# A mixer projection with the key block first and the values as 2x2 blocks: three of eight value pairs with seven products

## The chip, the cores and the metric

One Trainium2 chip, one of its cores. The metric is the device time of one call of the layer in microseconds, as the median of the runs. A profile of one more execution stands beside it; times inside the program are counted from the start of that profile's span.

## The reference

One encoder layer on 256 tokens of width 2048, all in float32. The change lies in the first part of the mixer, the projection of the normalised input by `w_mix_in` (2048 x 6656):

```
h = rms_norm(x, pre_norm_mix)
q_h, i_h, f_fwd, f_bwd, g_h, q_a, k_a, v_a = split(h @ w_mix_in)
#   columns: q_h 0, i_h 1024, f_fwd 2048, f_bwd 3072, g_h 4096 (1024 each),
#            q_a 5120 (1024), k_a 6144 (256), v_a 6400 (256)
y_h = hgrn2(q_h, i_h, f_fwd, f_bwd, g_h, ...)   # i_h: the values
y_a = window_attention(q_a, k_a, v_a, ...)      # keys and values of two heads
x = x + rms_norm(concat(y_h, y_a) @ w_mix_out, post_norm_mix)
```

Ahead of it and behind it stand a SwiGLU layer each (2048 to 2 x 5632 and back).

## The kernel before

**Products.** Every float32 matrix product is made of three products of rounded parts: each operand is split into a high part `h` and the remainder `l`, and `h*h`, `h*l` and `l*h` are summed in the same PSUM bank. Weights arrive as tiles `raw` of 128 x 2048 (1 MB, three buffers) on SP's queue. Each half of a tile is split by `split_half` (L171) through `split_act` (L176): ScalarE casts the half to `h` (L177), then VectorE subtracts, `l = raw - h` (L178). There are five buffers each for `h` and `l`, so a cast also waits until TensorE has left the half five before. A weight tile's buffer is loaded again once VectorE has made the last `l` from it.

**The input.** `xt` holds x times the gain, transposed, as 16 blocks of 128 rows of k with a high and a low part, in two tiles of eight blocks. It is not yet divided by the norm: the per-token factor `rs2` (one number per token, two columns for the token halves m = 0 and 1) is applied to results. Where a result has the tokens on partitions it is a scale of the eviction; where tokens lie along the free dimension, `spread` (L284) makes a 128 x 256 tile R with `rs2` along the free dimension by one product with a matrix of ones, and R is multiplied in. The two SwiGLU layers do more: `power_and_rest` splits `rs2` into a power of two and a rest, so that multiplying the second token half of `xt` by the exact ratio of the two powers ("evening", L1106) lets the halves be added to one another.

**The mixer's first stage.** The SwiGLU layer's `finish` already multiplies the first eight k-blocks of the first value group by weights that it loaded (`LeadN`: 512 columns from 1024). The mixer then runs, in this order: statistics of x (`pre_stats`) and the constants `lower_bounds`; the other eight blocks of that value group; the second value group (512 columns from 1536); 512 columns from 6144, which are k_a and v_a. These are plain products (`products_N`, L371): for each k-block and token half three products of 128 x 512, so 48 for half a group and 96 for a group. Then `headpair` (L1625) begins with the gates of head pair 0, with the weights as the stationary operand. The order of instructions is the scheduler's, by source order and readiness; `with tc.manual_schedule()` fixes it to the source's, for the engines named.

**Seven products.** `Blocks` (L418) can compute a pair u of k-blocks in another way: the 256 x 256 part of `xt` times the 256 x 1024 part of the weights is seen as 2 x 2 blocks and done with seven block products in place of eight (`seven`, L479), each of three parts. Its cost is sums: of weight blocks on VectorE (L486, L490, L492) between three splits of halves and one of a single block, and of `xt` blocks (`sums_of`, L406, and one split), kept in `sums`. Four partial products gather in banks of their own and are folded into the results at the end (`fold`, L530). The output projection by `w_mix_out` uses this for two of its eight pairs, the SwiGLU layers for many.

Of the kernel before, what the change touches and what calls it, by code (L numbers as in the profile page):

```python
# [11 lines left out]
F32 = mybir.dt.float32  # L12
F32R = mybir.dt.float32r
# [4 lines left out]
ALU = mybir.AluOpType  # L18
AX = mybir.AxisListType

P = 128
D = 2048
T = 256
# [14 lines left out]
def hymba_layer_kernel(  # L38
# [137 lines left out]
    def split_act(hi, lo, src):  # L176
        nc.scalar.copy(hi, src)  # L177
        nc.vector.tensor_tensor(lo, src, hi.bitcast(F32), ALU.subtract)  # L178
# [62 lines left out]
    def pre_stats():  # L241
        with tc.issue_after(last["act"].ins):
            pre_stats_now()
# [37 lines left out]
        nc.vector.tensor_scalar(rest[:, 1:2], rest[:, 1:2], two[:, 0:1], None, ALU.mult)  # L281
        nc.vector.tensor_copy(rest[:, 0:1], rs2[:, 0:1])

    def spread(factor=rs2, n=2):  # L284

        ps = pb()
        for m in range(n):
            nc.vector.tensor_scalar(
                R[:, m * P : (m + 1) * P], ident, factor[:, m : m + 1], None, ALU.mult
            )  # L290
        nc.tensor.matmul(ps[:, : n * P], ones, R[:, : n * P], start=True, stop=True)
        nc.vector.tensor_copy(R[:, : n * P], ps[:, : n * P])


    def xcol(xt, k, part=None):
# [313 lines left out]
    class Pairs(Blocks):  # L609
# [26 lines left out]
        def source(self, u):  # L636
            return Pairs.part(self.w, u, self.now)
# [12 lines left out]
        def left_sums(self, u):  # L650
            if self.ready and u in self.ready:
                return self.ready.pop(u)
            if u in self.kept:
                return self.kept[u]
            keep = self.now == 0 and u in self.keep
            if keep and u in self.near:
                w = self.room.tile([P, 4, 2, P], F32R, tag="sp", name=nm("sp"), bufs=3)
            else:
                tag = f"sp{u}" if keep else "sp"
                w = far["pool"].tile([P, 4, 2, P], F32R, tag=tag, name=nm("sp"), bufs=1 if keep else 2)  # L660
            split_act(w[:, :, 0, :], w[:, :, 1, :], self.sums[u])
            if keep:
                self.kept[u] = w
            return w
# [13 lines left out]
        def folded(self):  # L678
            if self.now == 0:
                wide = self.room.tile([P, 2, 512], F32, tag="sp", name=nm("y"), bufs=3)  # L680
                y = [
                    [
                        self.room.tile([P, 512], F32, tag="z", name=nm("y")),
                        self.room.tile([P, 512], F32, tag="s", name=nm("y")),
                    ],
                    [wide[:, i, :] for i in range(2)],
                ]
            else:
                t = self.post.tile([P, 2, 2, 512], F32, tag="tmp", name=nm("y"), bufs=1)
# [245 lines left out]
    def pair_of(xt, u):  # L935
        return xt[u // 4][:, u % 4 * 2 : u % 4 * 2 + 2]

    class Gated(Blocks):


# [127 lines left out]
    def ffn(gated, w_dn, post_gain, again, gain=None, lead=None, aside=None):  # L1068

        with ExitStack() as st:  # L1070
# [31 lines left out]

            def even(u):

                x = gated.tiles[u].rearrange("p k i t -> p (k i) t")[:, :, P:T]
                nc.vector.tensor_tensor(  # L1106
                    x, x.bitcast(F32), R[:, None, 0:P].to_broadcast([P, 4, P]), ALU.mult
                )

            def sums_in(u):  # L1110
                x = gated.tiles[u].bitcast(F32)
# [428 lines left out]
    def again_from(src):  # L1540
# [17 lines left out]
    cols = later["cols"]  # L1558
# [3 lines left out]
    with ExitStack() as s2:  # L1562
# [33 lines left out]
        w_in = w_mix_in[0]  # L1596
        vh = mid.tile([P, 2, 1024], F32, tag="vh", name="vh")
        for cg in range(2):
            sl = [pa(), pa()] if cg else vbanks
            if cg == 0:  # L1600
                pre_stats()
                with tc.issue_after(last["rs2"].ins):
                    lower_bounds()
            proj_N(w_in, 1024 + cg * 512, 512, xt, sl, k0=0 if cg else 8)
            for m in range(2):
                nc.scalar.mul(
                    vh[:, m, cg * 512 : (cg + 1) * 512], sl[m], rs2[:, m : m + 1]
                )

# [43 lines left out]
        va = mid.tile([P, 2, 256], F32, tag="va", name="va")  # L1653
        kz = mid.tile([P, 2, 256], F32, tag="q", name="kz")
        for m in range(2):
            nc.scalar.mul(kz[:, m, :], sl[m][:, :256], rs2[:, m : m + 1])
            nc.scalar.mul(va[:, m, :], sl[m][:, 256:], rs2[:, m : m + 1])
        kT = mid.tile([P, 2, T], F32, tag="kT", name="kT")

        def turned_keys():  # L1660
# [386 lines left out]
```

## Time and profile before

| | |
|---|---|
| median of 3 runs | 1821.23 us (1820.46 to 1823.14) |
| the profiled execution, time | 1822.32 us |
| its span | 1820.5 us |
| TensorE matmul / weight load busy | 1807.6 / 1501.9 us of the span |
| VectorE / ScalarE / GpSimd busy | 1604.3 / 1137.0 / 162.9 us |
| mixer's value and key groups in the span | about 703.7 to 772.8 us |
| DMA, mean over the span | 246 GB/s |

Matmul rows overlap in the pipeline: a 128 x 512 row lasts 389 ns but the next starts after about 227 ns, so durations are not added up; the distance of starts is. For VectorE and ScalarE, too, a row's end lies a little behind the next start when the next does not depend on it. "Idle before, releaser" is the time for which an engine stood before a row, and what ended it.

### The profile page before, as it was taken

What the parts mean: (1) busy time and instruction counts of PE and PEld (TensorE: products, weight loads), DVE (VectorE), ACT (ScalarE), POOL (GpSimd) and SP (SyncE); (2) the same over time, 40 slices, a digit from 0 to 9 for tenths busy, and PEclk for the clock granted to TensorE, in tenths of its full rate; (3) what the DMA queues carried; (4) which work ended last, traced back from release to release, by engine and by line L of the source; (5) the groups of instructions that cost most, each with busy time, mean ns of one, the idle gap of its engine ahead of it and who ended that gap; (6) DMA issues with size and microseconds to landing.
All of it is one profiled execution on the core that took longest, in us unless ns stands there. A gap on an engine that the chain in (4) does not pass through costs nothing.

```text
span 1820.5 us, 23469 instructions
## 1 busy us (share of the span) xinstructions
PE 1807.6 (99%) x8420; PEld 1501.9 (82%) x8420; DVE 1604.3 (88%) x2075; ACT 1137.0 (62%) x1508; POOL 162.9 (9%) x155
## 2 busy tenths in 40 slices
PE   9999999999999999999999999999999999999998
PEld 7888888888888888888888888888888888888886
DVE  7999999999989989477687798899999999999987
ACT  7565666666666657476587556656666666566663
POOL 1011111111011100000000000101111111011110
PEclk9999999999999999999999999999999999999999
DMA  8889999998699995655554456889999998699894
GB/s 302 236 238 285 276 283 256 249 265 249 218 342 271 294 307 189 199 180 176 165 174 149 164 208 239 253 246 265 281 276 267 256 249 249 193 345 302 265 317 157
DMA packets 212196, 447.59 MB, mean 246 GB/s; under 512 B 11768, under 2 KB 46928, under 8 KB 211312
## 3 DMA queue, kind: packets, MB, share of 16 engines
q1 hardware_dynamic: 180000, 384.87, 61.0%
q0 software_dynamic: 31904, 60.96, 19.5%
q8 instruction: 66, 1.08, 0.2%
q14 instruction: 50, 0.41, 0.1%
q10 hardware_dynamic: 176, 0.27, 0.0%
HBM read 433.46 MB, written 12.60 MB: 245 GB/s over the span
## 4 chain that ended last, share of the span: by engine, by line
PE 94%; DVE 2%; ACT 2%; DMA 1%; issue 1%; POOL 0%; DVEq 0%; ACTq 0%; POOLq 0%; SPq 0%
PE pa L454 41%; PE pb L454 35%; PE pa L322 5%; PE pa L327 3%; PE pa L377 2%; PE pa L375 2%; PE pa L376 2%; DMA raw<-in_w_ffn_gate_up_dram 1%; DVE l L178 1%; PE pa L1161 1%; PE pb L1161 1%; ACT h L177 0%; PE pb L1768 0%; PE pb L1742 0%; PE pb L1846 0%
## 5 line engine op out<-in xcount | busy, mean ns | idle before, releaser
L177 ACT CAST h<-raw 128x1024 fp32r<-128x1024 f32 (+1 forms) x867 | 855.1, 1013 | 466.8 <-PE pb L454 151.2
L178 DVE TENSOR_TENSOR l<-raw,h 128x1024 fp32r<-128x1024 f32 (+1 forms) x867 | 987.5, 1170 | 133.9 <-ACT h L177 99.7
L454 PE MATMUL pa<-h,xt 128*128 128x512 f32 x1096 | 384.6, 392 | 0.1
L454 PE MATMUL pb<-h,xt 128*128 128x512 f32 x940 | 336.7, 392 | 0.3 <-DVE pb L1218 0.3
L454 PEld LDWEIGHTS pa<-h,xt 128*128 128x128 f32 x1096 | 205.8, 188 | 44.1 <-DVE xt L233 0.6
L454 PE MATMUL pa<-l,xt 128*128 128x512 f32 x548 | 213.9, 390 | 0.0
L454 PEld LDWEIGHTS pb<-h,xt 128*128 128x128 f32 x940 | 176.4, 188 | 42.4 <-DVE pb L1225 3.6
L454 PE MATMUL pb<-l,xt 128*128 128x512 f32 x470 | 183.2, 390 | 0.0
L997 POOL DMA_DIRECT2D raw<-in_w_ffn_gate_up_dram x78 | 94.6, 1212 | 733.1 <-DVE l L178 642.2
L454 PE MATMUL pb<-h,ht 128*128 128x512 f32 x452 | 159.2, 389 | 0.0
L454 PE MATMUL pa<-h,ht 128*128 128x512 f32 x452 | 159.1, 389 | 0.0
L322 PE MATMUL pa<-xt,h 128*128 128x512 f32 x512 | 124.4, 393 | 0.2 <-ACT h L177 0.2
L454 PEld LDWEIGHTS pa<-l,xt 128*128 128x128 f32 x548 | 103.0, 188 | 20.7 <-DVE l L178 0.9
L454 PE MATMUL pa<-h,xs 128*128 128x512 f32 x312 | 111.6, 389 | 0.0
L322 PEld LDWEIGHTS pa<-xt,h 128*128 128x128 f32 x512 | 93.8, 188 | 18.6 <-ACT h L177 0.6
L454 PE MATMUL pb<-h,xs 128*128 128x512 f32 x312 | 108.7, 389 | 0.0
L454 PEld LDWEIGHTS pb<-l,xt 128*128 128x128 f32 x470 | 88.3, 188 | 16.7
L454 PEld LDWEIGHTS pb<-h,ht 128*128 128x128 f32 x452 | 84.9, 188 | 17.5
L454 PEld LDWEIGHTS pa<-h,ht 128*128 128x128 f32 x452 | 84.9, 188 | 17.5
L454 PE MATMUL pa<-l,ht 128*128 128x512 f32 x226 | 87.9, 389 | 0.0
L454 PE MATMUL pb<-l,ht 128*128 128x512 f32 x226 | 87.9, 389 | 0.0
L1303 POOL DMA_DIRECT2D raw<-in_w_ffn_down_dram x38 | 46.0, 1212 | 371.5 <-DVE la L178 311.3
(297 smaller groups left out, 2575.0 us busy)
## 6 DMA issues: line engine op xcount, KB each, us to landing
raw<-in_w_ffn_gate_up_dram SPq DMA_DIRECT2D x350, 512.0 KB, 5.7
raw<-in_w_ffn_down_dram SPq DMA_DIRECT2D x88, 1024.0 KB, 8.0
raw<-in_w_mix_in_dram SPq DMA_DIRECT2D x52, 1024.0 KB, 5.0
raw<-in_w_ffn_gate_up_dram POOLq DMA_DIRECT2D x78, 512.0 KB, 8.2
raw<-in_w_ffn_down_dram POOLq DMA_DIRECT2D x38, 512.0 KB, 10.1
raw<-in_w_mix_out_dram SPq DMA_DIRECT2D x16, 1024.0 KB, 4.9
ht<-away SPq DMA_DIRECT2D x24, 512.0 KB, 10.4
away<-ht SPq DMA_DIRECT2D x16, 512.0 KB, 6.9
```

Of the source, the lines that this page charges most:

```text
L177: nc.scalar.copy(hi, src)
L178: nc.vector.tensor_tensor(lo, src, hi.bitcast(F32), ALU.subtract)
L322: nc.tensor.matmul(slot[f], weights(hs, kk, f), xcol(xt, k), start=(k == 0), stop=(k == KT - 1))
L327: nc.tensor.matmul(slot[f][:, 0:T], weights(ls, kk, f), xcol(xt, kh * 8 + kk, 0), start=False, stop=False,)
L375: nc.tensor.matmul(dst, xh, h[:, o : o + n], start=(k == 0), stop=False)
L376: nc.tensor.matmul(dst, xh, l[:, o : o + n], start=False, stop=False)
L377: nc.tensor.matmul(dst, xl, h[:, o : o + n], start=False, stop=(k == KT - 1))
L454: nc.tensor.matmul(self.bank(at), lhs, rhs, start=(n == 1), stop=n in (ends, self.of[at]), skip_group_check=n > ends,)
L997: nc.gpsimd.dma_start(raw[:, 0:1024].rearrange("p (k c) -> p k c", k=2), self.source(u, g)[:, :, 1], accum_op=ALU.add,)
L1161: nc.tensor.transpose(bank[:, o : o + P], zs[m][:, k * P : (k + 1) * P], ident)
L1303: nc.gpsimd.dma_start(raws[i][:, 0:1024].rearrange("p (k c) -> p k c", k=2), Pairs.part(w_dn, u, r)[:, :, 512:1024], accum_op=ALU.add,)
```

## The change

The key block goes first. `LeadN` now loads and multiplies the 512 columns from 6144 (k_a and v_a), in banks called `kvbanks`; the mixer finishes that block (k-blocks 8 to 15) and evicts it to `kz` and `va`.

The values become one block of 1024 columns, as a class `Values(Blocks)` over eight pairs u = 0 to 7, in that order. Pairs 3, 5 and 6 are done with seven products, pairs 0, 1, 2, 4 and 7 plainly, and the partial products are folded in during pair 7.

For that, `xt` is evened in the mixer: `spread_begin(ratio, 1)` spreads the ratio of the two powers, `even` multiplies the second token half of each pair, and `value_sums` makes and splits the sums for pairs 3, 5 and 6. From then on the scale of results is `rest` in place of `rs2`: for the values, for R (`spread(rest)` after the values) and for `gates`. The statistics, `rsqrt`, `power_and_rest`, spreading, evening and the sums stand at places that the source gives: all of this lies in one `manual_schedule` block for TensorE, VectorE and ScalarE. `lower_bounds` comes after the last evening.

```diff
-    def spread(factor=rs2, n=2):
+    def spread_begin(factor, n=2):
         ps = pb()
...
         nc.tensor.matmul(ps[:, : n * P], ones, R[:, : n * P], start=True, stop=True)
-        nc.vector.tensor_copy(R[:, : n * P], ps[:, : n * P])
+        return ps[:, : n * P]
+
+    def spread(factor=rs2, n=2):
+        nc.vector.tensor_copy(R[:, : n * P], spread_begin(factor, n))
...
+    def even_half(x):
+        x = x.rearrange("p k i t -> p (k i) t")[:, :, P:T]
+        return nc.vector.tensor_tensor(
+            x, x.bitcast(F32), R[:, None, 0:P].to_broadcast([P, 4, P]), ALU.mult
+        )
...
-    vbanks = [pa(), pa()]
+    kvbanks = [pa(), pa()]
...
-        lead=LeadN(w_mix_in[0], 1024, vbanks),
+        lead=LeadN(w_mix_in[0], 6144, kvbanks),
...
-        for cg in range(2):
-            sl = [pa(), pa()] if cg else vbanks
-            if cg == 0:
-                pre_stats()
-                with tc.issue_after(last["rs2"].ins):
-                    lower_bounds()
-            proj_N(w_in, 1024 + cg * 512, 512, xt, sl, k0=0 if cg else 8)
+        class Values(Blocks):
...
+        def value_sums(u):
+            z, s = (keepy.tile([P, 4, P], F32, tag=f"sy{i}", name=nm("vs"), bufs=1) for i in range(2))
+            x = pair_of(xt, u).bitcast(F32)
+            whole = z.rearrange("p j t -> p (j t)").rearrange("p (k t) -> p k t", k=2)
+            nc.vector.tensor_tensor(whole, x[:, :, 0, :], x[:, :, 1, :], ALU.add)
+            w = keepy.tile([P, 4, 2, P], F32R, tag=f"yt{VALUES.index(u)}", name=nm("xs"), bufs=1)
+            split_act(w[:, :, 0, :], w[:, :, 1, :], sums_of(whole, s))
+            values.sums[u] = w
+
+        VALUES = (3, 5, 6)
...
+        with tc.manual_schedule(engines=ordered):
+            late = [load(source_N(w_in, 6144, 512, kc)) for kc in (2, 3)]
+            parts = [split(late[0]), ([], [])]
...
             for m in range(2):
-                nc.scalar.mul(
-                    vh[:, m, cg * 512 : (cg + 1) * 512], sl[m], rs2[:, m : m + 1]
-                )
+                for q in (2, 3):
+                    square_x(m, q)
+            rs = [rsqrt_of(squared.pop(m)[0], 1.0 / D, EPS) for m in range(2)]
+            next_half(0)
+            for m in range(2):
+                nc.vector.tensor_copy(rs2[:, m : m + 1], rs[m])
+            power_and_rest()
+            next_half(1)
+            values.begin(range(KT // 2))
+            raw = load(values.source(0))
+            kv(2, 0)
+            kv(2, 1)
+            kv(3, 0)
+            bank = spread_begin(ratio, 1)
+            first = [split_half(raw, 0)]
+            nc.vector.tensor_copy(R[:, :P], bank)
+            even(0)
+            first.append(split_half(raw, 1))
+            even(1)
+            kv(3, 1)
+            for m in range(2):
+                nc.scalar.mul(kz[:, m, :], kvbanks[m][:, :256], rs2[:, m : m + 1])
+                nc.scalar.mul(va[:, m, :], kvbanks[m][:, 256:], rs2[:, m : m + 1])
+            values.play(0, *zip(*first))
+            values.pos = 1
+            values.work(2)
+            even(2, 3)
+            value_sums(VALUES[0])
+            values.work(4)
+            even(4, 5)
+            values.work(5)
+            value_sums(VALUES[1])
+            values.work(6)
+            evened = even(6, 7)
+            for u in VALUES[2:]:
+                value_sums(u)
+            values.work(KT // 2)
+            for m in range(2):
+                for n in range(2):
+                    nc.scalar.mul(
+                        vh[:, m, n * 512 : (n + 1) * 512], values.c[m][n], rest[:, m : m + 1]
+                    )
+        spread(rest)
+        with tc.issue_after(evened.ins):
+            lower_bounds()
...
-        sl = [pa(), pa()]
-        for i, _ in enumerate(proj_N_pieces(w_in, 6144, 512, xt, sl)):
-            if i == 16:
-                spread()
...
-                by = rs2[:, m : m + 1]
+                by = rest[:, m : m + 1]
```

`Values` gives `Blocks` the columns 1024 to 2047 of `w_mix_in` as its source, the sums as `left_sums`, and four rooms for `fold`.

How the order of instructions moves, at two places. First VectorE, in the middle of the values. Before, between two evictions of the projection, its list there holds nothing but remainders of weight halves (`l`, from `raw` and `h`):

```order
L178 TENSOR_TENSOR l_6531<-raw_6528,h_6530 128x1024
L178 TENSOR_TENSOR l_6535<-raw_6528,h_6534 128x1024
L178 TENSOR_TENSOR l_6570<-raw_6567,h_6569 128x1024
L178 TENSOR_TENSOR l_6574<-raw_6567,h_6573 128x1024
L178 TENSOR_TENSOR l_6617<-raw_6614,h_6616 128x1024
```

Now, from the sums for pair 5 (`vs`, `xs`) through pair 5 (`raw_6535`) to the first block of pair 6 (`raw_6588`); L490, L494 and L496 are the sums of weight blocks, L945 the evening of two pairs, L1630 and L412 to L416 the sums of `xt`:

```order
L178 TENSOR_TENSOR xs_6529<-vs_6527,xs_6529 128x4x128
L178 TENSOR_TENSOR l_6538<-raw_6535,h_6537 128x512
L490 TENSOR_TENSOR raw_6535<-raw_6535 128x1024
L178 TENSOR_TENSOR l_6543<-raw_6535,h_6542 128x1024
L494 TENSOR_TENSOR raw_6535<-raw_6535 128x512
L178 TENSOR_TENSOR l_6548<-raw_6535,h_6547 128x1024
L496 TENSOR_TENSOR raw_6535<-raw_6535 128x512
L178 TENSOR_TENSOR l_6553<-raw_6535,h_6552 128x1024
L945 TENSOR_TENSOR xt_5939<-xt_5939,R 128x4x128 x2
L1630 TENSOR_TENSOR vs_6579<-xt_5939 128x512
```

What took two rows of 1024 per weight tile takes seven for a pair with seven products, with the evening and the sums of `xt` in the same list between pairs 5 and 6.

Second ScalarE, at the end of the key block. Before, the key block stood last, and its evictions (L1656, L1657) lay between casts for tiles far behind it:

```order
L177 CAST h_1203_6664<-raw_1202_6662 128x1024
L1656 ACTIVATE kz_6602<-pa_1171_6458,scales_111 128x256
L1657 ACTIVATE va_6601<-pa_1171_6458,scales_111 128x256
L177 CAST h_1205_6668<-raw_1202_6662 128x1024
L1656 ACTIVATE kz_6602<-pa_1172_6459,scales_111 128x256
L1657 ACTIVATE va_6601<-pa_1172_6459,scales_111 128x256
```

Now they stand after the casts for value pair 0 (`raw_1153`) and ahead of those for pair 1 (`raw_1159`); `xs_1166` is the sums' high part for pair 3, `raw_1167` pair 2:

```order
L177 CAST h_1157_6320<-raw_1153_6273 128x1024
L1682 ACTIVATE kz_6218<-pa_41_356,scales_111 128x256
L1683 ACTIVATE va_6217<-pa_41_356,scales_111 128x256
L1682 ACTIVATE kz_6218<-pa_42_357,scales_111 128x256
L1683 ACTIVATE va_6217<-pa_42_357,scales_111 128x256
L177 CAST h_1160_6367<-raw_1159_6365 128x1024
L177 CAST h_1162_6371<-raw_1159_6365 128x1024
L177 CAST xs_1166_6404<-vs_1165_6402 128x4x128
L177 CAST h_1168_6412<-raw_1167_6410 128x1024
```

All four evictions are together, and the casts of pair 1 are queued behind the last of them; the cast of the sums for pair 3 is queued ahead of the casts of pair 2.

More of the change, by code (lines that the diff above doesn't have):

```diff
@@ L1103, in even @@
             def even(u):
-                x = gated.tiles[u].rearrange("p k i t -> p (k i) t")[:, :, P:T]
-                nc.vector.tensor_tensor(
-                    x, x.bitcast(F32), R[:, None, 0:P].to_broadcast([P, 4, P]), ALU.mult
-                )
+                even_half(gated.tiles[u])
             def sums_in(u):
@@ L1597, in hymba_layer_kernel, with source, left_sums, folded @@
         vh = mid.tile([P, 2, 1024], F32, tag="vh", name="vh")
-        for cg in range(2):
-            sl = [pa(), pa()] if cg else vbanks
-            if cg == 0:
-                pre_stats()
-                with tc.issue_after(last["rs2"].ins):
-                    lower_bounds()
-            proj_N(w_in, 1024 + cg * 512, 512, xt, sl, k0=0 if cg else 8)
-            for m in range(2):
-                nc.scalar.mul(
-                    vh[:, m, cg * 512 : (cg + 1) * 512], sl[m], rs2[:, m : m + 1]
-                )
+        class Values(Blocks):
+            def source(self, u):
+                return Pairs.part(w_in, u, 1)
+            def left_sums(self, u):
+                return self.sums[u]
+            def folded(self):
+                return [
+                    [y[:, n, :] for n in range(2)]
+                    for y in (
+                        keepy.tile([P, 2, 512], F32, tag=f"yt{4 + m}", name=nm("y"), bufs=1)
+                        for m in range(2)
+                    )
+                ]
@@ new lines, in hymba_layer_kernel, with next_half, kv, even @@
+        VALUES = (3, 5, 6)
+        values = Values({u: pair_of(xt, u) for u in range(KT // 2)}, dict.fromkeys(VALUES))
+        va = mid.tile([P, 2, 256], F32, tag="va", name="va")
+        kz = mid.tile([P, 2, 256], F32, tag="q", name="kz")
+        ordered = {mybir.EngineType.PE, mybir.EngineType.DVE, mybir.EngineType.Activation}
+        with tc.manual_schedule(engines=ordered):
+            late = [load(source_N(w_in, 6144, 512, kc)) for kc in (2, 3)]
+            parts = [split(late[0]), ([], [])]
+            def next_half(i):
+                for part, of in zip(parts[1], split_half(late[1], i)):
+                    part.append(of)
+            def kv(kc, m):
+                hs, ls = parts[kc - 2]
+                for kk in range(4):
+                    products_N(
+                        xt, kvbanks, m, kc * 4 + kk, hs[kk // 2], ls[kk // 2], kk % 2 * 512, 512
+                    )
+            def even(*us):
+                for u in us:
+                    done = even_half(pair_of(xt, u))
+                return done
+            for m in range(2):
+                for q in (2, 3):
[39 more added lines that the diff above has]
+                        vh[:, m, n * 512 : (n + 1) * 512], values.c[m][n], rest[:, m : m + 1]
+                    )
@@ L1646, in headpair @@
             return z
-        sl = [pa(), pa()]
-        for i, _ in enumerate(proj_N_pieces(w_in, 6144, 512, xt, sl)):
-            if i == 16:
-                spread()
[L1653 to L1657, printed above, removed]
         kT = mid.tile([P, 2, T], F32, tag="kT", name="kT")
```

## The prediction

> **What bounds the kernel now.** First the page: the busy shares, the granted clock and the chain of waits.
>
> ```profile
> span 1820.5 us, 23469 instructions
> PE 1807.6 (99%) x8420; PEld 1501.9 (82%) x8420; DVE 1604.3 (88%) x2075; ACT 1137.0 (62%) x1508; POOL 162.9 (9%) x155
> PEclk9999999999999999999999999999999999999999
> PE 94%; DVE 2%; ACT 2%; DMA 1%; issue 1%; POOL 0%; DVEq 0%; ACTq 0%; POOLq 0%; SPq 0%
> ```
>
> TensorE is busy nearly all of the span at full clock, and 94% of the chain that ended last is its own work. So a product taken away is worth its place in the stream, and any wait put into that stream is paid in full. Next the windows of the changed stage: the end of the first value group, then everything up to the first head pair (columns: length, then busy time of TensorE, weight loads, VectorE, ScalarE, GpSimd, the clock, DMA share, GB/s). Then the groups of splits in this stretch.
>
> ```profile
> 717.80:728.90 11.10, 11.10 (x52) 9.20 (x51) 9.37 (x26) 9.97 (x22) 1.10 (x2) 1.00 0.89 285
> 728.90:772.80 43.90, 43.90 (x196) 36.35 (x195) 20.50 (x21) 20.48 (x22) 0.00 (x0) 1.00 0.61 199
> ...
> L178 DVE TENSOR_TENSOR l<-raw,h 128x1024 fp32r<-128x1024 f32 x22 | 26.8, 1223 | 23.7 <-ACT h L177 23.1
> L177 ACT CAST h<-raw 128x1024 fp32r<-128x1024 f32 x21 | 22.2, 1062 | 19.5 <-PE pa L377 19.5
> ```
>
> From 728.9 TensorE is busy without a gap for 43.9 us, while VectorE and ScalarE work under half of it. VectorE waits for casts and the casts wait for TensorE to release buffers: both run ahead as far as five buffers let them. This is the room that the change draws on.
>
> **What the change removes on TensorE.** The two value groups are 192 products of 128 x 512. Now five plain pairs make 5 x 24 = 120 and three pairs 3 x 21 = 63, so 183: nine fewer. The key block's 96 stay. The second window gives the pitch: 43.9 us for 192 products and one spread of about 0.3 is 0.227 each. Nine are **-2.04 us**. One spread of 128 columns is added:
>
> ```profile
> 1152.07 0.38 PE L291 MATMUL pb<-R,ones 128*128 128x128 f32 x2
> 1152.20 0.47 PE L454 MATMUL pb<-h,xt 128*128 128x512 f32 x1
> 1152.52 0.40 PE L454 MATMUL pb<-l,xt 128*128 128x512 f32 x1
> ```
>
> In the SwiGLU layer the same spread and the product behind it take 0.45 us where the product alone takes 0.23: **+0.22**. The product side gives -1.8 us; that is all there can be won.
>
> **What it adds on VectorE.** Rows of the same operations, from the output projection (a pair with seven products) and from the second SwiGLU layer (evening and sums):
>
> ```profile
> 1048.58 1.23 DVE L178 TENSOR_TENSOR l<-raw,h 128x1024 fp32r<-128x1024 f32 x1 [0.21 <-ACT h L177]
> 1049.72 1.22 DVE L486 TENSOR_TENSOR raw<-raw 128x1024 f32<-128x1024 f32 x1
> 1050.85 0.69 DVE L178 TENSOR_TENSOR sp<-sy,sp 128x512 fp32r<-128x512 f32 x1
> 1051.45 0.68 DVE L490 TENSOR_TENSOR raw<-raw 128x512 f32<-128x512 f32 x1
> 1052.11 1.23 DVE L178 TENSOR_TENSOR l<-raw,h 128x1024 fp32r<-128x1024 f32 x1
> 1053.25 0.69 DVE L492 TENSOR_TENSOR raw<-raw 128x512 f32<-128x512 f32 x1
> ...
> 1081.62 0.68 DVE L178 TENSOR_TENSOR la<-raw,ha 128x512 fp32r<-128x512 f32 x1
> 1082.34 1.22 DVE L486 TENSOR_TENSOR raw<-raw 128x1024 f32<-128x1024 f32 x1
> ...
> 1152.48 0.29 DVE L292 COPY R<-pb 128x128 f32<-128x128 f32 x1
> 1152.81 2.50 DVE L1106 TENSOR_TENSOR xt<-xt,R 128x512 fp32r<-128x512 f32 x4
> 1155.23 0.69 DVE L1113 TENSOR_TENSOR z<-xt 128x512 f32<-128x512 f32 x1
> 1156.43 0.42 DVE L408 TENSOR_TENSOR s<-z 128x256 f32<-128x256 f32 x1
> 1158.70 0.28 DVE L412 TENSOR_TENSOR s<-z,s 128x128 f32<-128x128 f32 x1
> 1158.91 1.22 DVE L178 TENSOR_TENSOR l<-raw,h 128x1024 fp32r<-128x1024 f32 x1
> ```
>
> From start to start a row of 1024 takes 1.13 us (1049.72 to 1050.85), one of 512 takes 0.60 (1050.85 to 1051.45), 256 about 0.34, 128 about 0.20 (1158.70 to 1158.91). A row that needs the one before takes 0.12 more (1081.62 to 1082.34).
>
> The list from the first evening to the last remainder of pair 6: eight evenings at 0.60, 4.8; eight halves of plain pairs (pair 0's second, two each of pairs 1, 2, 4, pair 7's first) at 1.13, 9.0; three pairs with seven products, each 0.60 for the first block, 1.13 + 0.60 + 0.60 for sums and 3 x 1.13 for halves, so 6.3, together 19.0; three sums of `xt` at 0.60 + 0.34 + 0.20 + 0.20 + 0.60 = 1.9, 5.8; the small rows of the bounds and one of R, about 0.7, my estimate from the 128 row. Together **39.3 us**.
>
> TensorE's need: the key block's remaining 48 products begin at 717.83,
>
> ```profile
> 717.83 0.48 PE L375 MATMUL pa<-h,xt 128*128 128x512 f32 x1
> ```
>
> so values begin at 717.83 + 10.9 + 0.2 = 728.9. The last remainder of pair 6 is read behind 154 value products, 34.9 us later, at 763.8. VectorE begins evening at about 727.0: the spread product cannot run before 726.0 (36 products in) and the copy of R takes 0.29 behind it, and VectorE's own queue (the split remainders 1.13 x 3 and some ten small statistics rows behind the last gain of `xt`) ends at the same point. It is done at 766.3 if it never waits: **2.5 us late**, from throughput alone.
>
> **The waits in that list.** These rows give the hand-offs:
>
> ```profile
> 773.00 0.47 ACT L1656 ACTIVATE kz<-pa,scales 128x256 f32<-128x256 f32 x1 [0.31 <-PE pa L377]
> 773.37 0.47 ACT L1657 ACTIVATE va<-pa,scales 128x256 f32<-128x256 f32 x1
> ...
> 1047.49 1.05 ACT L177 CAST h<-raw 128x1024 fp32r<-128x1024 f32 x1 [0.98 <-PE pa L454]
> 1054.03 1.05 ACT L177 CAST h<-raw 128x1024 fp32r<-128x1024 f32 x1 [1.00 <-DVE raw L492]
> ```
>
> A remainder starts 1.09 us after its cast of 1024 (1047.49 to 1048.58), a cast 0.1 after the sum that it waits for (1053.25 + 0.69 to 1054.03). So: (a) the casts of pair 1 stand behind the eviction of the key block's second half, which waits for its last product at 728.9; casts begin near 729.9, VectorE, done with pair 0 at 729.3, waits 1.6. (b) Each sum of `xt` sends VectorE to ScalarE and back (0.77), with the next pair's casts queued behind that cast (0.36), and three or four of its steps depend on the one before (0.36 to 0.48): pair 3 pays all of it, 1.6; for pair 5 the next cast stands ready, 1.1; for pair 6 the bounds' rows lie between the steps as well, 0.9. (c) In pairs 3 and 5 the last half is cast only after the last sum of weight blocks and nothing else stands in VectorE's list: 1.2 and two dependent steps, 1.45 each; pair 6 has pair 7's first half there, 0.1. Together 1.6 + 3.6 + 3.0 = **8.2 us**.
>
> TensorE then waits 2.5 + 8.2 = **10.7 us**. Laid out pair by pair, pairs 0 to 3 still arrive in time (pair 3's last remainder with some 0.9 us to spare), pair 4 is just late (0.2), pair 5 costs about 3, pair 6 about 7.5, with the longest single wait near 3 us at pair 6's first block. Pair 7's splits are then ready. None of it is made good later, since TensorE is never idle for want of anything but work.
>
> **Edits costed at nothing.** The statistics and the scale's split go ahead of the key block's last quarter on VectorE: that block's second half needs its remainder at about 725.0 and gets it at 724.8 to 725.2, so 0 to 0.3, and what it costs there is no longer missing later, since VectorE's list is what runs late. Loads: a tile of `w_mix_in` lands 5.0 us after its issue,
>
> ```profile
> raw<-in_w_mix_in_dram SPq DMA_DIRECT2D x52, 1024.0 KB, 5.0
> ```
>
> each is released by a remainder three tiles back, and pair 6's is issued when pair 3 is split, some 18 us before pair 6's casts; on SP's queue nothing but the same loads and the early bias rows stands ahead. Evictions of values, 4 x 0.69 on ScalarE, lie under the first head pair. The fold is eight rows of 0.60 on VectorE under pair 7 and the head pair; its first two results free the bank that the head pair's second product needs, by my layout 0.9 us before TensorE asks. If that cover is gone it costs up to 2.5 us (four rows of 0.60). The moved bounds cost ScalarE a table load in a stretch where it waits for VectorE's sums anyway.
>
> **Sum.** -2.04 + 0.22 + 10.7 = **+8.9 us**. Against the profiled execution's own 1822.32 us (span 1820.5 and 1.8 around it) that is 1831.2; against the median of the runs, 1.1 lower, 1821.2 + 8.9 = **1830.1 us**.
>
> Bounds of the unknown part, the waits in VectorE's list: none at all gives 2.5 us of waiting for TensorE; every hand-off at 0.1 more than taken (a dozen of them) and the fold uncovered give 10.7 + 1.2 + 2.5 = 14.4. I take 10.7, since each wait is read from the order of two in-order queues.
>
> **Rivals.**
>
> *The lead holds (not slower).* Mechanism: ScalarE and VectorE enter pair 4 far enough ahead that pairs 5 and 6 arrive in time. For it speaks the output projection, where VectorE is as full and TensorE never waits while a pair of seven is made:
>
> ```profile
> 1047.00:1056.00 9.00, 9.00 (x41) 7.47 (x40) 8.79 (x11) 5.08 (x6) 0.00 (x0) 1.00 0.63 234
> ```
>
> Against it: there the evening and most sums are absent, a plain pair lies between the two pairs with seven, and casts are not held by an eviction. It decides from the point where the lower remainder of pair 5 is ready by 756.4 (121 value products behind 728.9); my layout has it near 757.5. Then only the products count: 1821.2 - 1.8 = **1819.4**.
>
> *Throughput alone.* The queues interleave better than I lay them out and only the 2.5 us remain: 1821.2 - 1.8 + 2.5 = **1821.9**. Against it stand the fixed order in the manual block and the eviction ahead of pair 1's casts.
>
> *The clock drops in a wait.* The kernel's first five products come at a slow pace, and the only long wait of TensorE in the mixer leaves the clock at 1.00:
>
> ```profile
> 1.38 2.31 PE L129 MATMUL pb<-idle 128*128 128x512 bf16 x5 [1.38 <-DVE idle L123]
> ...
> 932.07 1.99 PE L1911 MATMUL pb<-pt,va 128*128 128x256 f32 x8 [0.84 <-ACT pt L1903]
> ...
> 930.00:934.00 4.00, 3.16 (x15) 2.40 (x14) 2.01 (x5) 3.97 (x6) 0.00 (x0) 1.00 0.00 0
> ```
>
> If the wait of 3 us at pair 6 has the effect of the program's start, about eight products come at (2.31 - 0.63) / 4 = 0.42 in place of 0.23 us: 1.5 us, **1831.6**. The Trainium skill (page "TensorE: Matmul & The Clock Gate", section "HAM oscillation — how this bites in real kernels") asks for no gap over about 3.4 us, since the array then runs at half rate; by that rule the wait lies just under the limit, and a drop would cost about 1.7 us as an estimate from its figures. No wait of that length is in this trace.
>
> *The backlog reaches the head pair.* The fold's rows stay behind TensorE and the second bank comes late: 1830.1 + 2.5 = **1832.6**. Against it: 0.9 us of margin.
>
> **How the numbers follow.** Forecast 0.67, lead holds 0.09, throughput alone 0.10, clock 0.06, backlog 0.08. What can be told from no change is about 0.2%, 3.6 us: 1817.6 to 1824.9. Faster than that needs the lead and luck on top: 0.02. Same: most of the first two rivals and the forecast's low end, 0.16. Slower 0.82. The forecast's own range is 1826 to 1833; with throughput alone and the upper bound (1821.2 - 1.8 + 14.4 = 1833.8) the range is 1821.5 to 1834.
>
> **What will show it.** In the new profile: 183 products between the key block and the first head pair; before them none or almost no wait of TensorE; in pairs 5 and 6 waits released by VectorE's `l` and ScalarE's `h`, 3 and 7 us in sum; VectorE over 80% busy from 727 to 774, with waits for `xs` and for the last `h` of pairs 3 and 5; ScalarE's casts of pair 1 right behind the second eviction. I am wrong if pair 5 arrives without a wait, if TensorE waits for a DMA there, or if the waits pass 14 us.

## The result, and the profile after

| | before | after |
|---|---|---|
| time, median of 6 runs | 1821.22 us (1820.46 to 1823.14) | 1832.19 us (1831.11 to 1834.51) |
| ratio | | 1.0058, 95% interval 1.0046 to 1.0071: slower by 0.6% |
| profiled execution: time, span | 1822.32, 1820.5 us | 1832.07, 1830.2 us |
| granted clock, mean | 0.999 | 0.996 |

The forecast was 1830.1 us, range 1821.5 to 1834.0. The page of the changed kernel, with the same four kinds of line as before (the span, the engines' busy time, the granted clock by slice, the shares of the chain of waits):

```profile
span 1830.2 us, 23528 instructions
PE 1811.9 (99%) x8413; PEld 1501.8 (82%) x8413; DVE 1633.9 (89%) x2129; ACT 1143.2 (62%) x1518; POOL 162.9 (9%) x155
PEclk9999999999999999899999999999999999999999
PE 92%; DVE 4%; ACT 2%; DMA 1%; issue 1%; POOL 0%; DVEq 0%; ACTq 0%; POOLq 0%
```

Two things are new: VectorE's share of the chain rose from 2% to 4%, and one slice of the clock shows an 8. Both lie in the value stage. The next rows are the windows of before, then of after, over the same stretch (length, busy time of TensorE, weight loads, VectorE, ScalarE and GpSimd, clock, DMA share, GB/s).

```profile
727.00:774.00 47.00, 47.00 (x209) 38.92 (x208) 22.50 (x28) 23.10 (x28) 0.45 (x1) 1.00 0.62 202
```

```profile
727.00:774.00 47.00, 40.87 (x159) 30.94 (x158) 39.77 (x58) 22.04 (x28) 0.00 (x0) 0.90 0.44 148
728.57:781.92 53.35, 47.22 (x184) 36.08 (x183) 46.08 (x67) 26.53 (x33) 0.00 (x0) 0.90 0.47 154
```

VectorE went from 22.5 to 39.8 of 47 us, 85%, and TensorE is no longer full. The last row is the whole value stage, from its first product to the second spread, with its 183 products. At the pitch of 0.227 us they need 41.5; the stage took 53.35. So TensorE lost **11.8 us** in it. Less the 1.8 that fewer products save, this is +10.0, against +9.75 between the two profiled executions and +10.97 between the medians.

"Lost" is meant like this for every kernel below: length of the stage less products x 0.227. TensorE's busy time in such a row does not serve, since the end of a matmul is modelled and slow products count as busy.

Who is waited for in this stage, first by TensorE (total, times, longest, in us), then the waits of VectorE in its own list (a timeline of the changed kernel: start, duration, what ran, and in brackets the idle time before it and its releaser):

```profile
PE pa L458 <- ACT h L177: 2.8, 1, 2.8
PE pa L458 <- DVE l L178: 2.3, 4, 0.8
PE pb L458 <- DVE l L178: 0.8, 1, 0.8
PE pb L458 <- ACT h L177: 0.3, 1, 0.3
```

```profile
730.59 2.36 DVE L178 TENSOR_TENSOR l<-raw,h 128x1024 fp32r<-128x1024 f32 x2 [1.83 <-ACT h L177]
...
736.67 0.69 DVE L178 TENSOR_TENSOR xs<-vs,xs 128x512 fp32r<-128x512 f32 x1 [0.69 <-ACT xs L177]
...
746.92 1.23 DVE L178 TENSOR_TENSOR l<-raw,h 128x1024 fp32r<-128x1024 f32 x1 [1.48 <-ACT h L177]
...
754.03 0.69 DVE L178 TENSOR_TENSOR xs<-vs,xs 128x512 fp32r<-128x512 f32 x1 [0.69 <-ACT xs L177]
...
761.37 1.23 DVE L178 TENSOR_TENSOR l<-raw,h 128x1024 fp32r<-128x1024 f32 x1 [1.19 <-ACT h L177]
...
766.31 0.69 DVE L178 TENSOR_TENSOR xs<-vs,xs 128x512 fp32r<-128x512 f32 x1 [0.68 <-ACT xs L177]
```

These are the hand-offs (a), (b) and (c) of the prediction, places where VectorE stands until ScalarE has made the cast that it needs. Each is where it was expected: pair 1's casts behind the eviction (1.83), three sums of `xt` (0.69, 0.69 and 0.68), the last halves of pairs 3 and 5 (1.48 and 1.19). No wait of TensorE or VectorE in this stage names a DMA.

The chain of work that ended last says the same. It leaves TensorE at 745.8 and comes back to it at 770.05, and between the two it runs over ScalarE and VectorE alone:

```profile
745.83 1.06 ACT h L177
...
768.86 1.15 DVE l L178
770.01 0.04 issue
770.05 3.78 PE pa L458 x8
```

TensorE's recorded waits add up to 6.2 us, not to 11.8. Most of the rest lies in its slow products, since a low clock, to which the prediction gave a chance of 0.06, came as well. TensorE's timeline at the start of pair 6, and the windows around it:

```profile
763.67 0.40 PE L458 MATMUL pb<-h,xt 128*128 128x512 f32 x1
766.85 0.79 PE L458 MATMUL pa<-h,xt 128*128 128x512 f32 x1 [2.78 <-ACT h L177]
767.66 0.80 PE L458 MATMUL pa<-l,xt 128*128 128x512 f32 x1
768.25 1.05 PE L458 MATMUL pa<-h,xt 128*128 128x512 f32 x2
770.05 0.80 PE L458 MATMUL pa<-l,xt 128*128 128x512 f32 x1 [0.75 <-DVE l L178]
...
771.07 0.63 PE L458 MATMUL pa<-h,xs 128*128 128x512 f32 x1
771.50 0.63 PE L458 MATMUL pa<-l,xs 128*128 128x512 f32 x1
...
775.31 0.40 PE L458 MATMUL pb<-l,xs 128*128 128x512 f32 x1
```

```profile
758.20:761.61 3.41, 2.88 (x12) 1.70 (x10) 2.22 (x4) 1.30 (x2) 0.00 (x0) 1.00 0.00 0
761.61:765.02 3.41, 1.70 (x6) 0.86 (x5) 3.41 (x8) 1.02 (x1) 0.00 (x0) 1.00 0.37 101
765.02:768.43 3.41, 1.57 (x3) 0.97 (x4) 2.69 (x7) 2.42 (x5) 0.00 (x0) 0.50 0.60 206
768.43:771.84 3.41, 2.66 (x7) 1.65 (x6) 3.41 (x6) 1.99 (x2) 0.00 (x0) 0.50 0.02 5
771.84:775.26 3.42, 3.42 (x9) 2.63 (x8) 3.42 (x6) 2.69 (x4) 0.00 (x0) 0.50 0.00 0
```

From 765.0 to 775.3 the granted clock is 0.50, and products start 0.43 us apart (771.07 to 771.50) where 0.227 was the pitch. The sixteen products from 766.85 to 775.31 took 8.5 us; at that pitch they would take 3.6. So two accounts of the 11.8 us stood open: VectorE's list is late, or the halved clock is the cost. The experiments begin there.

### The profile page after: what moved, and what is told of

It reads as the page before. It is cut to its first block, busy times and chain, and to the rows that moved or that the text cites. A ratio compares the mean times of both kernels' runs of the same rounds, so it can differ in the third digit from the quotient of the medians.

```text
span 1830.2 us, 23528 instructions
## 1 busy us (share of the span) xinstructions
PE 1811.9 (99%) x8413; PEld 1501.8 (82%) x8413; DVE 1633.9 (89%) x2129; ACT 1143.2 (62%) x1518; POOL 162.9 (9%) x155
## 4 chain that ended last, share of the span: by engine, by line
PE 92%; DVE 4%; ACT 2%; DMA 1%; issue 1%; POOL 0%; DVEq 0%; ACTq 0%; POOLq 0%
PE pa L458 41%; PE pb L458 36%; PE pa L326 5%; PE pa L331 3%; DVE l L178 2%; PE pa L381 1%; PE pa L380 1%; PE pa L379 1%; DMA raw<-in_w_ffn_down_dram 1%; PE pa L1169 1%; PE pb L1169 1%; ACT h L177 0%; PE pb L1856 0%; PE pb L1830 0%; PE pb L1934 0%
## 5 line engine op out<-in xcount | busy, mean ns | idle before, releaser
L458 PE MATMUL pa<-h,xt 128*128 128x512 f32 x1148 | 403.8, 393 | 2.9 <-ACT h L177 2.8
L458 PE MATMUL pb<-h,xt 128*128 128x512 f32 x986 | 352.8, 392 | 0.0
L458 PEld LDWEIGHTS pa<-h,xt 128*128 128x128 f32 x1148 | 216.1, 188 | 49.3 <-ACT h L177 3.2
L458 PE MATMUL pa<-l,xt 128*128 128x512 f32 x574 | 225.1, 392 | 2.1 <-DVE l L178 2.1
L458 PEld LDWEIGHTS pb<-h,xt 128*128 128x128 f32 x986 | 185.1, 188 | 44.0 <-DVE pb L1233 3.5
L458 PE MATMUL pb<-l,xt 128*128 128x512 f32 x493 | 192.2, 390 | 0.0
L458 PEld LDWEIGHTS pa<-l,xt 128*128 128x128 f32 x574 | 108.1, 188 | 25.7 <-DVE l L178 5.1
L458 PE MATMUL pa<-h,xs 128*128 128x512 f32 x324 | 116.7, 392 | 0.0
L458 PE MATMUL pb<-h,xs 128*128 128x512 f32 x324 | 113.8, 391 | 0.3 <-ACT h L177 0.3
```

The source lines that it names most:

```text
L458: nc.tensor.matmul(self.bank(at), lhs, rhs, start=(n == 1), stop=n in (ends, self.of[at]), skip_group_check=n > ends,)
```

## The experiments

Eleven kernels, each run beside the kernel before. The "lost" column is stage length less products x 0.227; the last column is the difference of medians.

| kernel | products | stage, us | lost, us | median, us | to its own before, us |
|---|---|---|---|---|---|
| the change | 183 | 53.35 | 11.8 | 1832.19 | +11.0 |
| e1, no pair of seven | 192 | 43.53 | 0 | 1822.46 | +0.5 |
| e2, pairs 3 and 6 | 186 | 44.35 | 2.1 | 1823.42 | +1.5 |
| e3, evictions later | 183 | 51.16 | 9.6 | 1830.35 | +8.4 |
| e4, evenings in the hand-offs | 183 | 50.95 | 9.4 | 1830.79 | +8.8 |
| e5, zero products in the wait | 183 + 12 | 53.09 | 11.5 | 1833.20 | +11.6 |
| e6, sums on GpSimd | 183 | 56.80 | 15.3 | 1835.97 | +14.4 |
| e7, sums and evenings on GpSimd | 183 | 53.03 | 11.5 | 1830.98 | +9.4 |
| e8, e3 and e4 together | 183 | 49.11 | 7.6 | 1827.40 | +5.8 |
| e9, e2 with both edits | 186 | 42.17 | 0 | 1821.45 | -0.6 |
| e10, four evenings less | 183 | 50.58 | 9.0 | 1829.25 | +7.2 |
| e11, e7 without its wait for R | 183 | 53.34 | 11.8 | 1831.63 | +9.6 |

### e5: is it the clock?

```diff
+            for _ in range(12):
+                nc.tensor.matmul(
+                    values.c[0][0],
+                    none,
+                    values.sums[5].rearrange("p j i t -> p (j i t)")[:, 0:512],
+                    start=False, stop=False,
+                )
             values.work(KT // 2)
```

`none` is a block of zeros.

> Twelve products of a zero block are put into TensorE's queue between pair 5 and pair 6 (2.7 us at 0.227), where the change waits 2.78 us; they add zero to a bank. Theory (the data of pair 6 comes late, and the slow products only pass time that TensorE would wait anyway; with the clock at 1.00 its last remainder would be used 0.4 us earlier): 1832.2 - 0.4 = 1831.8, and TensorE still waits inside pair 6. Rival E (the halved clock is the cost): 16 products at 0.43 in place of 0.227 us are 3.2 us, so 1829.0.

Measured: 1833.2 us, ratio 1.0065 (1.0048 to 1.0081). The stage of this kernel, and rows of TensorE's timeline in it:

```profile
727.74:780.83 53.09, 47.44 (x196) 35.97 (x195) 45.85 (x67) 26.53 (x33) 0.00 (x0) 1.00 0.47 154
```

```profile
763.11 2.97 PE L1700 MATMUL pa<-xs,none 128*128 128x512 f32 x12
...
769.24 0.50 PE L458 MATMUL pa<-l,xt 128*128 128x512 f32 x1 [1.43 <-DVE l L178]
...
774.12 0.50 PE L458 MATMUL pb<-l,xs 128*128 128x512 f32 x1 [0.76 <-DVE l L178]
```

The long wait is filled, the clock stays at 1.00 through the whole stage, and the stage is shorter by 0.26 us. The filling itself delayed nothing: pair 6's first product came 38.3 us behind the first of the stage in both kernels. So 0.26 us is what the halved clock cost here, by one profile of each kernel: at full speed TensorE reaches each next remainder sooner and waits for it instead (1.43 and 0.76 in these rows). Rival E, 3.2 us, falls. The median did not get better at all.

### e1, e2: which part of the change costs it?

```diff
-        VALUES = (3, 5, 6)
+        VALUES = ()          # e1
+        VALUES = (3, 6)      # e2
```

The calls of `value_sums` follow the list.

> No pair with seven products; the key block first, the spread and the eight evenings stay. Theory (VectorE's list is too long by the sums and hand-offs of the sevens): the list loses 3 x 6.3 + 5.8 and gains six halves of 1.13, about 21 us in place of 39.3, so TensorE never waits in the value stage: 192 products and the spread, 1821.2 + 0.2 = 1821.4 us. Rival A (the new order or the evening costs by itself): 1824 to 1828, with waits of TensorE released by xt or by the eviction.

> Sevens in pairs 3 and 6 alone, two plain pairs between them. Theory: the list falls by 6.3 + 1.9 - 2.3 = 5.9 us, which is more than the 2.5 us that it was late, and the hand-offs of one pair go too; a wait of about 1 us is left at pair 6: 1821.2 - 1.36 + 0.22 + 1.0 = 1821.1 us. Rival B (every pair with seven products costs the same, a third of what the change costs): 2 x (10.97 - 0.22) / 3 = 7.2 more than 1821.4: 1828.6. Rival C (the low clock in the long wait is the cost): no wait over 1 us, clock 1.00 throughout, and the time falls by the whole of it, to 1820.

Measured: e1 1822.46 us, ratio 1.0003 (0.9994 to 1.0012); e2 1823.42, ratio 1.0009 (0.9999 to 1.0018). The stages of e1 and of e2 by windows:

```profile
727.64:771.17 43.53, 43.53 (x194) 36.04 (x193) 25.45 (x32) 22.47 (x26) 0.00 (x0) 1.00 0.66 219
```

```profile
729.54:773.89 44.35, 43.01 (x187) 34.76 (x186) 39.18 (x57) 24.23 (x30) 0.00 (x0) 1.00 0.56 184
```

With the key block first, the statistics ahead of it, the spread and all eight evenings, but no pair of seven, TensorE loses nothing: rival A falls. Two pairs of seven with two plain ones between lose 2.1 us, where a third of the change's loss for each would be 7.9: rival B falls too. So does rival C: in e2 the clock is 1.00 and no wait is over 0.8 us, yet the time is not 1820. The loss is not so much for each such pair; it follows what VectorE has to do in the stage: 39.18 us busy in e2 and 46.08 in the change (row 728.57:781.92), while the products need 42.2 and 41.5. The theory's wait of 1.0 for e2 was too low by 1.1, and its 1821.1 us by 2.3.

### e3, e4, e8: the hand-offs

```diff
             kv(3, 1)
-            for m in range(2):
-                nc.scalar.mul(kz[:, m, :], ...)
-                nc.scalar.mul(va[:, m, :], ...)
             values.play(0, *zip(*first))
             values.pos = 1
             values.work(2)
+            for m in range(2):                       # e3
+                nc.scalar.mul(kz[:, m, :], ...)
+                nc.scalar.mul(va[:, m, :], ...)
```

```diff
-            values.work(4)
-            even(4, 5)
+            values.work(3)
+            with_hole(3, 4, 5)     # e4: pair 3, with even(4, 5) ahead of its last half
             values.work(5)
             value_sums(VALUES[1])
-            values.work(6)
-            evened = even(6, 7)
+            evened = with_hole(5, 6, 7)
```

> Key and value evictions stand behind the casts of pair 1 on ScalarE; all else as in the change. Theory: VectorE's wait of 1.83 us at 730.6 goes, the rest of its list moves up by as much, and TensorE's waits in pairs 4 to 6 fall from 11.7 to about 10: 1832.2 - 1.8 = 1830.4. Rival D (throughput or the buffers set it, the wait is taken again further on): 1832 with the same 11.7.

> The evenings of tiles 4, 5 and 6, 7 stand ahead of the last remainder of pairs 3 and 5 on VectorE, so the hand-off to ScalarE (waits of 1.48 and 1.19 us) has work in it. Theory: 1.2 us each are saved, TensorE's waits fall from 11.7 to about 9.3: 1832.2 - 2.4 = 1829.8. Rival D: the same time as the change, 1832, since the last remainder of pair 5 now comes later by two rows of 0.60.

> The edits of the evictions and of the evenings in one kernel. Alone they shortened the value stage by 2.2 and 2.4 us. Theory: they act at different places of VectorE's list, but pair 3's hand-off no longer lies on the path once the casts come early, so less than the sum: 3.5 to 4.6 us off, 1828.2, with waits of about 7.5 left. Rival D (the same wait is removed by both): 1830.

Measured: e3 1830.35 us, ratio 1.0044 (1.0029 to 1.0059); e4 1830.79, 1.0048 (1.0031 to 1.0065); e8 1827.40, 1.0033 (1.0021 to 1.0045). In the stage e3 wins 2.2 us, e4 2.4, and e8 4.2 of their sum of 4.6. The theory had 1.8, 2.4 and 3.5 to 4.6; the median of e4 came out 1.0 above its forecast, while its stage is as forecast. Each hand-off that is hidden comes back to TensorE nearly whole, further down its stream: VectorE's list is late from pair 4 on, and whatever shortens it shortens the end. Rival D falls.

### e10: four rows less on VectorE

```diff
-            even(2, 3)
...
-            even(4, 5)
```

This kernel leaves out the evening of four of the eight pairs, so its values are not the layer's.

> The evenings of tiles 2 to 5 are left out (the second half of the rows keeps its own scale there), four rows of 0.60 on VectorE and nothing else; every hand-off between the queues stays. Theory (VectorE's list is late from pair 4 on, so each row in it is paid): TensorE's waits fall by 4 x 0.60 = 2.4 from 11.8 to 9.4, 1829.8. Rival I (only the hand-offs set the waits and VectorE has slack between them): the rows are taken up by longer waits for casts, 1832.2. Rival A' (ScalarE's casts wait for TensorE's buffers, so that VectorE's time is worth half): 1831.0.

Measured: 1829.25 us, ratio 1.0043 (1.0027 to 1.0058); the stage is 2.8 us shorter for four rows of 0.60. No hand-off was touched, so rows count as much as waits do, and rivals I and A' fall. It is 0.4 more than the rows; where that came from was not followed up.

### e6, e7, e11: the rows on GpSimd

```diff
-    def sums_of(u, w):
+    def sums_of(u, w, on=nc.vector):
...
-            nc.vector.tensor_tensor(whole, x[:, :, 0, :], x[:, :, 1, :], ALU.add)
+            nc.gpsimd.tensor_tensor(whole, x[:, :, 0, :], x[:, :, 1, :], ALU.add)
...
-                    done = even_half(pair_of(xt, u))                       # e7, e11
+                    done = even_half(pair_of(xt, u), nc.vector if u < 2 else nc.gpsimd)
...
-        spread(rest)                                                       # e11
-        with tc.issue_after(evened.ins):
+        with tc.issue_after(evened.ins):    # here the last remainder of a sum
+            spread(rest)
             lower_bounds()
```

The three other rows of `sums_of` go to GpSimd in the same way, in all three kernels.

> The four rows of each sum of xt stand on GpSimd in place of VectorE; the casts and remainders stay. GpSimd's one row of 128x512 took 1.27 us, VectorE's 0.60. Theory (the order of two in-order queues sets the waits): a sum takes 3.0 us in place of 1.6, ScalarE's cast of it comes later and the casts of the next weights stand behind it, so VectorE waits longer and TensorE's waits rise from 11.8 to 12 to 13: 1833. Rival F (only the length of VectorE's list counts): 5.1 us fewer rows, waits of 6.7, 1827.

> The evenings of tiles 2 to 7 and all sums of xt stand on GpSimd, which is otherwise idle here. They begin at 726.3 and take about 6 x 1.3 + 3 x 2.6 = 15.6 us, so each is done before ScalarE comes to its cast, except the first, at pair 3. Theory: VectorE's list falls from 39.3 by 5.1 + 3.6 to about 30 us, 35 are there; the hand-offs are hidden but for pair 3's; waits of TensorE of 1 to 3 us at pair 6 and none at pair 5: 1821.2 - 1.8 + 2 = 1821.4. Rival G (GpSimd and VectorE slow each other down, so that the rows on either take half as long again): VectorE's rows of 1.13 become longer and the waits stay over 6 us: over 1826.

> As the kernel with evenings and sums on GpSimd, but the second spread and the bounds are issued behind the last remainder of a sum, so that VectorE's queue no longer holds a row that writes R behind GpSimd's reading of it (6.01 us of VectorE's time there). Theory (the shared rows stay slow: 1.22 became 2.3 on VectorE and 1.28 became 2.2 on GpSimd while both worked): the first sum still ends at about 737, so some 2.5 of the 6 us are won: 1828.4. Rival J (the wait for R alone made that kernel slow): waits of 5 to 6 us go, 1825. Rival K (nothing is won, since ScalarE's cast of the first sum comes as late as before): 1831.

Measured: e6 1835.97 us, ratio 1.0077 (1.0062 to 1.0092); e7 1830.98, 1.0051 (1.0036 to 1.0066); e11 1831.63, 1.0054 (1.0040 to 1.0068). All three missed the theory's numbers. e6 lost 15.3 us, more than the 12 to 13 expected; rival F's 6.7 falls. VectorE's wait at pair 3's sum, 0.69 in the change, is 4.02 there:

```profile
737.26 0.69 DVE L178 TENSOR_TENSOR xs<-vs,xs 128x512 fp32r<-128x512 f32 x1 [4.02 <-ACT xs L177]
```

For e7 the theory had 1821.4, and rival G, over 1826, was right. Rows of VectorE and of GpSimd in e7 while both worked:

```profile
725.43 0.69 DVE L945 TENSOR_TENSOR xt<-xt,R 128x512 fp32r<-128x512 f32 x1
726.04 2.32 DVE L178 TENSOR_TENSOR l<-raw,h 128x1024 fp32r<-128x1024 f32 x1
728.27 1.78 DVE L945 TENSOR_TENSOR xt<-xt,R 128x512 fp32r<-128x512 f32 x1
...
737.25 0.46 DVE L288 TENSOR_SCALAR R<-ident,scales 128x128 f32<-128x128 f32 x1 [6.01 <-POOL xt L945]
```

```profile
725.54 5.67 POOL L945 TENSOR_TENSOR xt<-xt,R 128x512 fp32r<-128x512 f32 x3 [5.27 <-DVE lb L1601]
731.17 1.28 POOL L1630 TENSOR_TENSOR vs<-xt 128x512 f32<-128x512 f32 x1
```

Alone, VectorE's remainder takes 1.22 us and the evening 0.69; here 2.32 and 1.78, longer by 1.10 and 1.09, close to one GpSimd row of 1.28 less what overlaps. GpSimd's three evenings take 5.67 where 3 x 1.28 would be 3.8. The two engines take turns on these rows, so where they meet a row given to GpSimd costs VectorE more than the 0.60 that it saved. The Trainium skill (page "SBUF — State Buffer", section "Who interferes with whom") has a rule for this: a VectorE instruction with two SBUF inputs contends with a GpSimd instruction that reads SBUF, for a shared pair of ports that is an exclusive lock. By that rule these rows come out as sums, and the trace agrees (2.32 for 1.13 and 1.28); the number expected for e7 had not reckoned with it.

On top of that VectorE stood 6.0 us behind a row that rewrites `R`. e11 took that wait away, and its stage is no shorter (53.34). The first sum of `xt` now ended even later on GpSimd, ScalarE's casts were queued behind it, and VectorE stood 5.83 us at the sum's remainder instead:

```profile
740.67 1.21 DVE L178 TENSOR_TENSOR xs<-vs,xs 128x512 fp32r<-128x512 f32 x1 [5.83 <-ACT xs L177]
```

Rival K was right there, and rival J falls.

### e9: what is left if the list fits

e2 with the edit of e3, and the evenings of tiles 4 and 5 in pair 3's hand-off.

> Sevens in pairs 3 and 6 alone, the evictions behind the casts of pair 1, the evenings of tiles 4 and 5 in pair 3's hand-off. With the sevens in 3 and 6 alone TensorE still waited 2.1 us (stage of 44.35 less 186 x 0.227). Theory: the two edits took 2.2 and 2.4 us off a list that was late throughout; here 2.1 are left to take, so no waits: 2.1 us under the 1823.4 of the kernel without them, 1821.3, beside the 1821.2 to 1822.0 of the kernel before: no difference that can be told. Rival H (products taken off are won in full once no wait is left, 6 x 0.227 - 0.22 = 1.1 us): 0.06% faster than before, 1820.6.

Measured: 1821.45 us, ratio 0.9996 (0.9988 to 1.0005). Its stage:

```profile
729.41:771.58 42.17, 42.17 (x188) 34.91 (x187) 39.45 (x57) 23.19 (x30) 0.00 (x0) 1.00 0.59 201
```

VectorE is 94% busy and TensorE loses nothing: 186 x 0.227 is 42.2. This is the version that keeps what is won, but the 1.1 us (0.06%) that the products give is not told from no change, so rival H stays undecided. It beats the change by far; that it beats the kernel before is not shown.

## Why the prediction was right

- **Products.** 183 between the key block and the first head pair, and with no waits (e9, e1) the stage is products x 0.227 to within 0.1 us. -2.04 and +0.22 hold as they stand.
- **Start.** Values were to begin at 728.9 and began at 728.57; in front of them TensorE was busy for 26.85 of 27 us (700 to 727) before and after. Statistics ahead of the last quarter cost nothing, as costed.
- **VectorE's list.** First evening at 726.3 (forecast 727.0), end of pair 6's last remainder at about 774.8 (forecast 727.0 + 39.3 + 8.2 = 774.5). That the end fits so well is in part luck: the list began 0.7 earlier than forecast and took 1.0 longer.
- **(a)** forecast 1.6, measured 1.83, and taken away in e3 it gave 2.2. **(b)** forecast 1.6, 1.1 and 0.9 with the dependent steps: measured 1.6, 1.15 and 0.8, from start to start less the rows' own time; the bare waits are 0.69 at each sum and 0.26 at the cast behind the first. **(c)** forecast 1.45, 1.45 and 0.1 with the dependent steps: the bare waits are 1.48, 1.19 and none. Pair 3's is 0.29 longer for a reason that the forecast had not named: its last cast was released at 745.83 by TensorE, which left a buffer then, and not by the sum of weight blocks, which was done about 0.4 before.
- **TensorE's waits by pair**, each pair counted from the end of the one before, less what its products need: pairs 0 to 3 none, pair 4 0.8 (forecast 0.2), pair 5 3.2 (3), pair 6 7.8 (7.5), pair 7 none. The longest single one is 2.8 (near 3), at pair 6's first block, as said.
- **Costed at nothing.** TensorE and VectorE waited for no load. ScalarE did once, 3.25 us up to 780.2, with casts for the head pair behind the values, and TensorE did not wait after it. The fold stayed covered: from 782 to 830 TensorE has no recorded wait, so the backlog rival (1832.6) was near in time and wrong in mechanism.
- **The rivals.** The lead did not hold. Throughput alone did not describe it: hidden hand-offs gave their time back (e8, 4.2 us). The clock rival was half right: the clock fell, at the place named, to 0.50. But its price was worked out from the slow products (1.5 us) as if TensorE had its data; it did not, and e5 puts the price at 0.26. The step that failed is that one: a slow product inside a wait costs only what goes beyond the wait.

The sum was 10.7 of waits and 11.8 came: 0.6 at pair 4, 0.2 at pair 5, 0.3 at pair 6, the last about what the clock cost. The other part of the distance from 1830.1 to 1832.2 lies in the step from profiled runs to medians: the profiled execution of before was 1.1 above its median, that of after 0.1 below.

## What to carry to other kernels

Half-idle is an average: before a change is put under the cover of a busy engine, write down the in-order list of the covering engine up to the last deadline, with every hand-off to another queue in it, and compare its end with the time at which it is needed. Once such a list is late, rows and hand-offs alike are paid in full further on, and the cure is less work in it (two pairs of seven in place of three) or other rows inside the hand-offs, not a faster product side. A helper engine has to be quick enough for the queue behind it (e6), and its rows must not exclude those of the engine that it relieves (e7).

## What the hardware showed beyond that

**The clock changes by stretches of 3.41 us, not by single gaps.** In the change it fell at 765.0 and came back at 775.3, 10.24 us later. In e4, where the longest wait was 1.57 us, it fell as well, at 766.39, while a product ran, and came back 6.83 later. It fell in this stage in eight of the twelve changed kernels, for 3.41 us (e11), 6.83 (e4, e6, e7, e8, e10) or 10.24 (the change, e3): once, twice or three times 3.41. The two windows of e4 ahead of the fall and the first behind it:

```profile
759.57:762.98 3.41, 2.31 (x9) 1.24 (x7) 3.41 (x8) 2.20 (x2) 0.00 (x0) 1.00 0.02 5
762.98:766.39 3.41, 1.54 (x6) 0.67 (x4) 2.69 (x7) 2.42 (x5) 0.00 (x0) 1.00 0.89 303
766.39:769.80 3.41, 2.01 (x5) 1.49 (x5) 3.41 (x6) 1.99 (x2) 0.00 (x0) 0.50 0.02 5
```

TensorE was busy for 1.54 of 3.41 us in the stretch that ended with the fall (1.70 in the change, 0 to 1.74 in the other six); 2.31 and 2.88 in the stretches ahead let it stand, and so did 1.92 in e6 (762.73 to 766.15). So about half of a stretch fits as the limit, as an estimate from these figures. One stretch of e11, the first of these, does not fit:

```profile
737.47:740.88 3.41, 1.53 (x7) 0.94 (x5) 0.21 (x1) 0.86 (x2) 3.33 (x5) 1.00 0.51 210
740.88:744.30 3.42, 1.74 (x6) 1.23 (x7) 3.42 (x3) 3.12 (x4) 2.65 (x3) 1.00 0.01 2
744.30:747.71 3.41, 3.41 (x9) 2.63 (x8) 3.38 (x4) 0.64 (x1) 3.25 (x3) 0.50 0.55 150
```

There 1.53 let the clock stand, and only the 1.74 behind it brought it down. Why is open: the ends of products are modelled, so these shares are rough, and no run set them on purpose. The way back is plainer: in all eight kernels the clock rose behind a stretch in which TensorE was busy throughout (3.42 in the change, where 2.66 in the stretch ahead was not enough).

The rule of the Trainium skill that the prediction named (page "TensorE: Matmul & The Clock Gate", section "HAM oscillation — how this bites in real kernels"), no gap over about 3.4 us, was too mild for the change and e4: their longest recorded waits were 2.78 and 1.57 us and the clock fell all the same, so the measurement decides.

**GpSimd and VectorE take turns** on the rows with two inputs shown at e7: 2.32 us for a row of 1.22. No run here set rows with one input against them.
